# K tile 1 of the first projection is issued from ACT's queue instead of SP's

## The chip, the cores and the metric

One Trainium2 chip, one core of it. The metric is the device time of one execution in microseconds (us), the median of several runs. The kernel before takes 143.43 us (three runs, 143.29 to 143.65).

PE is the matrix engine (TensorE; PEld its weight loads), DVE the vector engine, ACT the scalar engine, POOL GpSimd, SP the engine that issues most DMAs. The small q behind an engine's name (SPq, ACTq, POOLq) marks its sequencer, which issues DMAs, waits for semaphores and hands instructions to the engine.

## The reference

One layer of a hybrid decoder with 256 tokens of width 1024, in float32:

```
h = rms_norm(x, norm_g)
mq, mk, mv, mg, dq, dk, dv, dg = split(h @ w_in)          # eight chunks of 512 columns
m_out = block_attention(norm(mq), norm(mk), mv) * silu(mg) # 8 heads of 64, ALiBi, causal
d_out = rms_norm(diff_attention(norm(dq), norm(dk), dv)) * 0.8 * silu(dg)
x + concat(m_out, d_out) @ w_out
```

## The kernel before

The input is used transposed: eight k tiles of 128 rows, each 256 columns wide (the tokens). Every float32 operand is split into a high and a low part (`whi`, `wlo` for weights, `xhi`, `xlo` for the input), and each product is three matmuls: high by high, high by low, low by high (`PASSES`). The order of all work is written out by hand in the table `ORDER`: steps `x.0` to `x.7` split the first eight k tiles, `u.0` to `u.7` are the matmuls of the first chunk (dq), one k tile each, `h.`, `l.` and `L.` split and load the later weights, the rest is attention and the output projection.

The first chunk comes in with the input. Array `xw` holds for each k tile 128 rows with 256 columns of x and 512 columns of dq's weights. The x part of tile 0 lies in the array `small_x` beside the norm gains, and is the first DMA of all (L103). Tile 0's weights come in two halves of 256 columns (L110), tiles 1 to 7 whole, 768 columns, 384 KB each (L112). All DMAs are issued by SP, in the order of the code. Of the DMAs that the names DMAHW0 to DMAHW7 stand for, in rotation, a later one that takes the same name waits for the earlier one to land.

For every tile kt, `split_first` does this: DVE (for tiles 3, 5, 7 ACT) makes `xhi` (L156 or L154), DVE makes `xlo` (L157), ACT makes `whi` (L265), DVE makes `wlo` (L266); tile 0's weights go in two halves. Then `unit_nat` issues the matmuls (L293): tile 0 twelve of 256 columns, the other tiles six of 512.

Ahead of them stand a memset on DVE (L124) and one exponential on ACT (L125), which brings in ACT's table, and seven warm-up matmuls on zeros (L131; each is two instructions). Two more of these, the fillers, stand behind the matmuls of tile 0. POOL meanwhile makes eight bias tiles (L144).

Behind dq come the chunks dk, dv and so on, whose weights are loaded by `load_w` (L250) into three buffers and split at L273 and L277.

Of the kernel before, what the change touches and what calls it, by code (L numbers as in the profile page):

```python
# [55 lines left out]
def kernel(  # L56
# [9 lines left out]
    nc = tc.nc  # L66
# [12 lines left out]
    def bank(name):  # L79
        tag = free_banks.pop(0)  # L80
        t = psum.tile([P, 512], F32, tag=tag, name=name)
        bank_of[id(t)] = (tag, t)
        return t
# [7 lines left out]
    def tile768(name):  # L91
        tag = free_tiles.pop(0)
        t = work.tile([P, 768], F32, tag=tag, bufs=1, name=name)
        tile_of[id(t)] = (tag, t)
        return t
# [9 lines left out]
    first = []  # L105
    for kt in range(KT):
        t = tile768("first")
        if kt == 0:
            for c in (slice(S, 512), slice(512, 768)):
                nc.sync.dma_start(out=t[:, c], in_=xw[kt][:, c])  # L110
        else:
            nc.sync.dma_start(out=t, in_=xw[kt][:, 0:768])  # L112
        first.append(t)
    xn = const.tile([P, 2, D], F32, name="xn")
# [8 lines left out]
    warm = const.tile([P, 1], F32, name="warm")  # L123
    nc.vector.memset(warm, 0.0)  # L124
    nc.scalar.activation(out=warm, in_=warm, func=AF.Exp)  # L125
    zero = nc.const_aps.tensor(0.0, [P, 512], F32)
    wps = bank("warm_ps")

# [566 lines left out]
```

## Time and profile before

| what | us |
|---|---|
| median of three runs | 143.43 |
| the profiled execution, its own time | 142.81 |
| its span, first to last instruction | 141.0 |
| PE busy | 137.1 (97%) |
| DVE busy | 105.8 (75%) |
| ACT busy | 84.2 (60%) |
| POOL busy | 23.3 (17%) |
| DMA, mean over the span | 173 GB/s |

The profiled execution's own time holds its span and 1.8 us around it. The profile page gives for each engine the union of its instructions' times; the chain of waits is followed back from the last instruction; the timeline lists an engine's instructions in order, merged where they stand on one line, and in brackets the idle time before each and what ended it. Times are us from the start of the span. A merged row's time reaches from the first start to the last end; matmuls overlap, so their pitch is read from one start to the next.

### The profile page before, as it was taken

How to read it: one execution, taken by the hardware profiler on the slowest of the kernel's cores; microseconds unless marked ns; L12 is line 12 of the kernel's file. 1: busy time of each engine (PE TensorE's matmuls, PEld its weight loads, DVE VectorE, ACT ScalarE, POOL GpSimd, SP SyncE). 2: the span in 40 equal slices, each digit the busy share in tenths (PEclk: the TensorE clock that was granted, in tenths of full speed). 3: DMA queues.
4: the chain of work that ended last, by engine and by line, in shares of the span. 5: the costliest groups of instructions: out<-in, count | busy, mean ns of one | idle time of the engine just before them, and what ended most of it. 6: DMA issues, size and time to landing. Idle time of an engine off the chain costs nothing.

```text
span 141.0 us, 2227 instructions
## 1 busy us (share of the span) xinstructions
PE 137.1 (97%) x806; PEld 116.5 (83%) x806; DVE 105.8 (75%) x249; ACT 84.2 (60%) x167; POOL 23.3 (17%) x28
## 2 busy tenths in 40 slices
PE   7999999999999999999999999999999999999991
PEld 7978888887888888888877888888999888898890
DVE  1799985989995998997999999994529435692331
ACT  4378893694292998945640599799768504670000
POOL 7970000000000000000000000279760007000000
PEclk9999999999999999999999999999999999999999
DMA  5999999571809600268960004916144800000232
GB/s 117 303 410 413 409 426 407 237 246 56 297 0 316 281 2 0 30 272 293 328 274 0 0 0 121 414 65 225 72 112 191 297 0 0 7 0 0 81 142 74
DMA packets 5482, 24.39 MB, mean 173 GB/s; under 512 B 608, under 2 KB 1376, under 8 KB 3424
## 3 DMA queue, kind: packets, MB, share of 16 engines
q1 hardware_dynamic: 5472, 24.26, 47.3%
q8 instruction: 6, 0.10, 0.3%
q14 instruction: 4, 0.03, 0.1%
HBM read 23.21 MB, written 1.05 MB: 172 GB/s over the span
## 4 chain that ended last, share of the span: by engine, by line
PE 97%; DVE 0%; issue 0%
PE oacc L602 16%; PE acc_dq L293 9%; PE acc_mg L308 8%; PE acc_mq L293 8%; PE acc_dg L293 8%; PE acc_mk L293 8%; PE acc_dv L293 8%; PE acc_mv L293 8%; PE acc_dk L293 8%; PE s_ps L413 4%; PE T_ps L318 3%; PE warm_ps L131 3%; PE mo_ps L495 2%; PE do_ps L501 1%; PE aT_ps L473 1%; PE aT_ps L471 1%
## 5 line engine op out<-in xcount | busy, mean ns | idle before, releaser
L277 DVE TENSOR_TENSOR wlo<-w,whi 128x1024 fp32r<-128x1024 f32 x36 | 43.5, 1232 | 6.0 <-ACT whi L273 5.7
L273 ACT ACTIVATE whi<-w 128x1024 fp32r<-128x1024 f32 x36 | 36.4, 1057 | 4.4 <-DMA w<-w 4.1
L443 POOL TENSOR_TENSOR p<-p,rs 128x512 f32<-128x512 f32 (+1 forms) x8 | 8.3, 1064 | 82.0 <-DVE rs L439 81.7
L433 ACT ACTIVATE p<-p,nmax 128x256 f32<-128x256 f32 (+1 forms) x32 | 14.1, 443 | 3.9 <-DVE nmax L423 3.9
L423 DVE CUSTOM_DVE_ANT_0 p<-s_ps,bias 128x256 f32<-128x256 f32 (+1 forms) x32 | 9.1, 351 | 1.8 <-PE s_ps L413 1.8
L602 PE MATMUL oacc<-whi,mixm 128*128 128x512 f32 (+1 forms) x40 | 10.4, 347 | 0.0
L602 PE MATMUL oacc<-whi,mixd 128*128 128x512 f32 (+1 forms) x40 | 10.4, 346 | 0.0
L308 PE MATMUL acc_mg<-xhi,whi 128*128 128x256 f32 x32 | 9.2, 289 | 0.0
L308 PE MATMUL acc_mg<-xlo,whi 128*128 128x256 f32 x32 | 9.0, 281 | 0.0
L308 PE MATMUL acc_mg<-xhi,wlo 128*128 128x256 f32 x32 | 9.0, 281 | 0.0
L609 DVE TENSOR_TENSOR o<-oacc,xn 128x512 f32<-128x512 f32 (+1 forms) x5 | 2.9, 585 | 7.7 <-PE oacc L602 7.7
L602 PEld LDWEIGHTS oacc<-whi,mixm 128*128 128x128 f32 x40 | 7.1, 189 | 1.0
L602 PEld LDWEIGHTS oacc<-whi,mixd 128*128 128x128 f32 x40 | 7.0, 188 | 1.0
L144 POOL TENSOR_SCALAR bias<-dist 128x256 f32<-128x256 f32 x8 | 7.3, 922 | 0.4
L265 ACT ACTIVATE whi<-first 128x512 fp32r<-128x512 f32 (+1 forms) x9 | 5.0, 577 | 3.7 <-DMA first<-xw 3.7
L602 PE MATMUL oacc<-wlo,mixd 128*128 128x512 f32 (+1 forms) x20 | 6.9, 347 | 0.0
L602 PE MATMUL oacc<-wlo,mixm 128*128 128x512 f32 (+1 forms) x20 | 6.9, 347 | 0.0
L479 ACT ACTIVATE pT<-aT_ps 128x512 f32<-128x512 f32 x6 | 3.6, 594 | 5.4 <-PE aT_ps L472 5.4
L293 PE MATMUL acc_mk<-whi,xhi 128*128 128x512 f32 x16 | 6.7, 418 | 0.0
L293 PE MATMUL acc_mv<-whi,xhi 128*128 128x512 f32 x16 | 6.5, 405 | 0.0
L293 PE MATMUL acc_dv<-whi,xhi 128*128 128x512 f32 x16 | 6.5, 405 | 0.0
L293 PE MATMUL acc_dg<-whi,xhi 128*128 128x512 f32 x16 | 6.5, 404 | 0.0
(167 smaller groups left out, 352.8 us busy)
## 6 DMA issues: line engine op xcount, KB each, us to landing
w<-w SPq DMA_DIRECT2D x16, 1024.0 KB, 4.9
first<-xw SPq DMA_DIRECT2D x7, 384.0 KB, 5.7
w<-w SPq DMA_DIRECT2D x4, 512.0 KB, 8.5
xn<-x SPq DMA_DIRECT2D x2, 512.0 KB, 9.5
out<-o SPq DMA_DIRECT2D x3, 256.0 KB, 2.1
first<-xw SPq DMA_DIRECT2D x2, 128.0 KB, 2.6
out<-o SPq DMA_DIRECT2D x2, 128.0 KB, 1.7
small<-small_x SPq DMA_DIRECT2D x1, 136.0 KB, 2.3
```

The source lines that it names most:

```text
L131: nc.tensor.matmul(wps[:, 0:P], lhsT=zero[:, 0:P], rhs=zero[:, 0:P], start=True, stop=True)
L144: nc.gpsimd.tensor_scalar(out=b, in0=dist, scalar1=2.0 ** -(h + 1), scalar2=None, op0=ALU.mult)
L265: nc.scalar.activation(out=hi[:, c], in_=src, func=AF.Copy)
L273: nc.scalar.activation(out=piece(i)[0], in_=raw_half(i), func=AF.Copy)
L277: nc.vector.tensor_tensor(out=lo, in0=raw_half(i), in1=hi.bitcast(F32), op=ALU.subtract)
L293: nc.tensor.matmul(acc[name][t][:, o:o + n], lhsT=(xhi, xlo)[a][:, kt, t * P:(t + 1) * P], rhs=wp[b][:, c:c + n], start=kt == 0 and i == 0 ...
L308: nc.tensor.matmul(acc[name][j // 2][:, (j % 2) * S:(j % 2 + 1) * S], lhsT=wp[b][:, c:c + P], rhs=(xhi, xlo)[a][:, kt], start=kt == 0 and ...
L413: nc.tensor.matmul(ps[c][k][:, o:o + n], lhsT=qk[g + "q"][a][rows, pr, q0:q0 + P], rhs=qk[g + "k"][b][rows, pr, 0:n], start=i == 0, stop=i ...
L423: nc.vector.tensor_tensor_reduce(out=p[:, o:o + n], in0=s_ps[g][c][k][:, b:b + n], in1=biases[c][:, S - n:], scale=-1.0, scalar=3.0e38, op ...
L433: nc.scalar.activation(out=p[:, o:o + n], in_=p[:, o:o + n], func=AF.Exp, scale=-1.0, bias=mx[:, i:i + 1], accum_out=sums[g, pr][:, i:i + 1])
L443: nc.gpsimd.tensor_tensor(out=p3, in0=p3, in1=q.unsqueeze(2).to_broadcast([P, 2, n]), op=ALU.mult)
L602: nc.tensor.matmul(acc["o", c][j][:, 0:n], lhsT=qk[g][a][:, kt, t * P:(t + 1) * P], rhs=pieces[piece][b][:, o:o + n], start=first and i == ...
```

## The change

SP no longer issues tile 1; ACT does, on its own queue. In the code the issue stands behind the exponential of L125. SP issues tile 2 where it issued tile 1 before, and each later tile one place earlier.

```diff
         if kt == 0:
             for c in (slice(S, 512), slice(512, 768)):
                 nc.sync.dma_start(out=t[:, c], in_=xw[kt][:, c])
-        else:
+        elif kt > 1:
             nc.sync.dma_start(out=t, in_=xw[kt][:, 0:768])
         first.append(t)
...
     nc.vector.memset(warm, 0.0)
     nc.scalar.activation(out=warm, in_=warm, func=AF.Exp)
+    nc.scalar.dma_start(out=first[1], in_=xw[1][:, 0:768])
     zero = nc.const_aps.tensor(0.0, [P, 512], F32)
```

Lines from 126 on stand one further down in the changed kernel.

ACT's instructions from the start of the program, before; `warm` is the scratch value of the exponential, `first` a k tile, and in brackets stands what an instruction waits for (DVE_49 is a count of DVE's work, DMAHW1_49 the landing of the DMA with that name):

```order
L125 ACT_TABLE_LOAD
L125 ACTIVATE warm<-warm 128x1 [waits DVE_49]
L265 ACTIVATE whi<-first 128x256 [waits DMAHW1_49]
L265 ACTIVATE whi<-first 128x256 [waits DMAHW2_49]
L265 ACTIVATE whi<-first 128x512 [waits DMAHW3_49]
L265 ACTIVATE whi<-first 128x512 [waits DMAHW4_49]
```

The same place in the changed kernel:

```order
L125 ACT_TABLE_LOAD
L125 ACTIVATE warm<-warm 128x1 [waits DVE_49]
L126 DMA first<-xw 128x768
L266 ACTIVATE whi<-first 128x256 [waits DMAHW1_49]
L266 ACTIVATE whi<-first 128x256 [waits DMAHW2_49]
L266 ACTIVATE whi<-first 128x512 [waits DMAHW4_49]
L266 ACTIVATE whi<-first 128x512 [waits DMAHW3_49]
```

The DMA is the third instruction and waits for nothing of its own. Tile 1 now has the name DMAHW4, tile 2 DMAHW3.

SP's DMAs from the start of the program, before:

```order
L103 DMA small<-small_x 128x272
L110 DMA first<-xw 128x256 x2
L112 DMA first<-xw 128x768 x5
L112 DMA first<-xw 128x768 [waits DMAHW0_49]
L112 DMA first<-xw 128x768 [waits DMAHW1_49]
L250 DMA w_172<-w 128x1024 [waits DMAHW2_49]
L250 DMA w_172<-w 128x1024 [waits DMAHW3_49]
L250 DMA w_175<-w 128x1024 [waits DMAHW4_49]
```

And in the changed kernel:

```order
L103 DMA small<-small_x 128x272
L110 DMA first<-xw 128x256 x2
L112 DMA first<-xw 128x768 x4
L112 DMA first<-xw 128x768 [waits DMAHW0_49]
L112 DMA first<-xw 128x768 [waits DMAHW1_49]
L251 DMA w_172<-w 128x1024 [waits DMAHW2_49]
L251 DMA w_172<-w 128x1024 [waits DMAHW3_49]
L251 DMA w_175<-w 128x1024 [waits DMAHW4_49]
```

SP issues one tile less. The second half of the first w load waits for DMAHW3, which was tile 1 and is tile 2 now; the next one waits for DMAHW4, which was tile 2 and is tile 1 now.

## Rows read from the trace of the kernel before

**Rows 1.** Stretches: length, busy PE, PEld, DVE, ACT, POOL, granted clock, DMA share, GB/s.
```profile
16.78:137.89 121.11, 121.07 (x734) 102.93 (x733) 92.64 (x225) 73.63 (x151) 14.66 (x12) 1.00 0.42 154
```

**Rows 2.** The chain of waits, first 18 us: start, length, what.
```profile
0.75 3.32 PE warm_ps L131 x14
...
6.58 10.20 PE acc_dq L293 x42
```

**Rows 3.** PE's timeline: start, length, engine, line, operation, count.
```profile
4.39 0.63 PE L293 MATMUL acc_dq<-whi,xlo 128*128 128x256 f32 x2
4.82 0.56 PE L293 MATMUL acc_dq<-wlo,xhi 128*128 128x256 f32 x2
...
5.72 0.40 PE L293 MATMUL acc_dq<-wlo,xhi 128*128 128x256 f32 x2
5.96 0.61 PE L131 MATMUL warm_ps<-const-float32-0.0 128*128 128x128 f32 x4
...
6.29 0.27 PE L131 MATMUL warm_ps<-const-float32-0.0 128*128 128x128 f32 x1
6.58 0.73 PE L293 MATMUL acc_dq<-whi,xhi 128*128 128x512 f32 x2
...
9.62 0.62 PE L293 MATMUL acc_dq<-whi,xhi 128*128 128x512 f32 x2
...
12.42 0.39 PE L293 MATMUL acc_dq<-whi,xhi 128*128 128x512 f32 x1
```

**Rows 4.** Waits of PE's weight loads, first 18 us: total, times, longest.
```profile
PEld acc_dq L293 <- DVE wlo L266: 0.5, 2, 0.3
PEld acc_dq L293 <- ACT whi L265: 0.2, 1, 0.2
```

**Rows 5.** DVE's timeline, first 8 us.
```profile
0.79 0.06 DVE L124 MEMSET warm<- 128x1 f32 x1 [0.79 <-PEq L687]
...
5.91 0.37 DVE L156 TENSOR_SCALAR xhi<-first,small 128x256 fp32r<-128x256 f32 x1 [0.35 <-DMA first<-xw]
...
6.71 0.88 DVE L266 TENSOR_TENSOR wlo<-first,whi 128x512 fp32r<-128x512 f32 x1
```

**Rows 6.** ACT's timeline, first 8 us.
```profile
0.71 1.28 ACT L125 ACT_TABLE_LOAD   x1 [0.71 <-PEq L687]
2.00 0.20 ACT L125 ACTIVATE warm<-warm 128x1 f32<-128x1 f32 x1
...
5.90 0.63 ACT L265 ACTIVATE whi<-first 128x512 fp32r<-128x512 f32 x1 [0.81 <-DMA first<-xw]
7.37 0.63 ACT L265 ACTIVATE whi<-first 128x512 fp32r<-128x512 f32 x1 [0.84 <-DMA first<-xw]
```

**Rows 7.** L691's sequencer step (ns; first and last start, us) and ACT's timeline, late.
```profile
L691 ACTq DRAIN  x2: 14/1900/3787, 122.2 to 140.6; - x2
122.04 3.89 ACT L273 ACTIVATE whi<-w 128x1024 fp32r<-128x1024 f32 x4
98.01 1.28 ACT L582 ACT_TABLE_LOAD   x1
99.31 1.27 ACT L582 ACTIVATE sg<-acc_dg,r 128x512 f32<-128x512 f32 x2
```

**Rows 8.** SP's issues of tiles 1 to 7, and tile 1's us from issue to landing.
```profile
2.08 3.60 SPq L112 DMA_DIRECT2D first<-xw  x7
first<-xw SPq DMA_DIRECT2D x1, 384.0 KB, 3.8
```

**Rows 9.** Busy time by stretches, columns as in rows 1.
```profile
1.50:4.50 3.00, 3.00 (x16) 2.99 (x15) 1.47 (x3) 1.11 (x3) 2.84 (x5) 1.00 0.89 203
6.58:16.78 10.20, 10.20 (x43) 7.96 (x44) 10.10 (x19) 7.58 (x12) 2.99 (x4) 1.00 1.03 411
```

**Rows 10.** Timelines of DVE and PE at the first w load.
```profile
14.82 3.64 DVE L277 TENSOR_TENSOR wlo<-w,whi 128x1024 fp32r<-128x1024 f32 x3
16.85 0.39 PE L293 MATMUL acc_dk<-wlo,xhi 128*128 128x512 f32 x1
```

## The prediction, made before the change was run

> **What bounds the kernel now.** TensorE (PE) is busy 97% of the span; the table by stretches says where the rest is: from 16.78 to 137.89 us PE works 121.07 of 121.11 us [rows 1], so no later wait can take up a shift. What the first 16.78 us gain or lose, the end gains or loses. The chain of waits there is PE alone: the warm-up matmuls to 4.07 us, tile 0 of dq, two fillers, and then 10.20 us for tiles 1 to 7 [rows 2]. In PE's timeline a pair of 512-wide matmuls takes 0.467 us once things run (six pairs from 9.62 to 12.42 us), while tiles 1 and 2, six pairs too, take from 6.58 to 9.62 us, 3.04 us instead of 2.80 [rows 3]. The waits of PE's weight loads name the holes: 0.2 us for tile 1's high half (ACT, L265), 0.5 us for two low halves (DVE, L266) [rows 4].
>
> Behind both stands one transfer. DVE ends tile 0 at 5.56 us and then sits 0.35 us until tile 1 has landed, which it starts at 5.91 us [rows 5]; ACT starts tile 1's high half at 5.90 us after 0.81 us idle for a DMA [rows 6]. DVE's three steps for tile 1 follow each other to 7.59 us and those of tile 2 come straight behind, so the delay is handed on.
>
> **The prize.** PE's fillers start 0.11 us apart (three steps from 5.96 to 6.29 us), so PE could go on at 6.40 us instead of 6.58: 0.18 us. The holes in tiles 1 and 2 are 3.04 - 2.80 = 0.24 us. Together 0.42 us, all that an early tile 1 can give as long as tile 0 comes when it does now. An early tile 1 does close them: with DVE on tile 1 straight from 5.56 us, its steps (5.91 to 7.59 us now, 1.68 us [rows 5]) end at 7.24 us, and PE, from 6.40 us, wants the low half two pairs later, at 7.33 us.
>
> **When ACT issues it.** The new instruction stands third in ACT's stream, behind the table load (0.71 to 1.99 us) and the exponential (2.00 to 2.20 us) [rows 6]. What counts is whether ACT's sequencer waits for these two to end. The trace says no. At the end of the program ACT's sequencer starts its closing DRAIN at 122.2 us, and it lasts 3787 ns, while four activations of L273 run from 122.04 to 125.93 us [rows 7]: the sequencer had passed three that had not begun. And the activation behind the second table load starts at 99.31 us, 0.02 us after the load's end: it had been handed over before. The exponential waits only for DVE's memset, done at 0.85 us [rows 5]. So the issue falls near 0.9 us, beside SP's issues of small and tile 0, which end before 2.08 us [rows 8], and not at 2.20 us. An issue took SP 0.51 us (seven in 3.60); ACT's next work waits for tile 0 to land, so the issue costs ACT nothing.
>
> **When tile 1 lands then.** From SP's queue it took 3.8 us from issue to landing, behind small and tile 0 [rows 8]. If it takes as long, it lands at 4.7 us; with a queue of its own it can only be earlier than that by the part that it spent behind them. DVE wants it at 5.56 us: hidden, with 0.86 us of cover. Tile 2 takes tile 1's place in SP's issue, one issue earlier than now, and should land before the 7.37 us at which ACT starts it now; DVE then waits neither in tile 1 nor in tile 2.
>
> **What it takes from tile 0.** Tile 1's 384 KB now move beside small and tile 0, 392 KB. From both sides: if they fit into idle capacity, tile 0 is not late at all: from 1.50 to 4.50 us the engines moved 203 GB/s against 411 later [rows 9], so 3.0 us x 208 = 624 KB were free, more than the 393 KB (thousand bytes) wanted; against that, the engines counted as busy for 0.89 of it, with packets that waited. If all of tile 1 goes ahead, tile 0 is late by 393 KB / 411 GB/s = 0.96 us. The first half of tile 0 will feel it more: I take 0.6 us there, PE's first real matmul at about 4.4 us instead of 3.8. PE then has two pairs at the early pitch of 0.43 us (4.39 to 4.82) and four at the later one of 0.24 (5.72 to 5.96) [rows 3], done at 4.4 + 0.86 + 0.96 = 6.2 us where now the fillers begin at 5.96. So 0.2 us, nearer the lower end because the bytes leave room. DVE's low half of tile 0's second half may come as much late, beside it and not on top.
>
> [...] No row here shows two loading queues at once. [...]
>
> Of the rest: the bytes and the computing instructions stay the same. SP's later issues wait for other landings: the second half of the first w load for tile 2 instead of tile 1, the next one for tile 1 instead of tile 2. They are not near: the low half of the very first w tile starts on DVE at 14.82 us and takes 1.2 us (three in 3.64), and PE asks for it at 16.85 us [rows 10], 0.8 us of cover, more than the 0.42 us that PE can come earlier. With that cover gone PE would wait for DVE at the first dk tile.
>
> **The sum.** -0.18 - 0.24 + 0.2 = -0.22 us: 142.81 becomes 142.6 us for a profiled execution like this one. That execution lies 0.62 us under the median of the runs (143.43), so the median becomes 143.2 us. With tile 0 late by 0 to 0.96 us it is 143.0 to 144.0 us. What a measurement of this kernel can tell from no change is about 0.3%, 0.43 us: the whole prize has that size, and my forecast is a difference that can't be told.
>
> **Rival 1, slower: the issue does wait for the table load and the exponential.** Then it starts at 2.20 us, 0.12 us later than now (2.08 us [rows 8]), while tile 2 is issued at 2.08 us on the other queue and moves beside it. PE reaches tile 1 between 0.12 us later than now and the time at which both have come, where now tile 2's high half starts: 7.37 - 5.90 = 1.47 us [rows 6]. I take 1.2, nearer the upper end: two tiles asked for at the same time share the engines, and these counted as busy for 0.89 of the time even with one [rows 9]. DVE's chain moves along whole, so nothing is won back: 144.0 us, 144.6 on the median's scale. It decides from an issue at about 1.76 us on: 3.8 us later, at 5.56 us, DVE wants the tile. For it: the order in the code. Against it: rows 7. Chance 0.17.
>
> **Rival 2, slower: the clock.** [...] Chance 0.08.
>
> **Rival 3, faster: tile 0 is not late at all**, or even earlier, as its last packets no longer have tile 1 behind them in SP's queue. Then 0.42 us or a little more: 142.4 us, or 143.0 and less on the median's scale. For it: the free bytes [rows 9]. Chance 0.10.
>
> **How the numbers follow.** The forecast has 0.65, its own range 143.0 to 144.0 us. Faster by over 0.3%: most of rival 3 and the lowest part of the forecast, 0.19. Slower: rivals 1 and 2 nearly whole and the uppermost part of the forecast, 0.27. Within: 0.54. The range reaches down to 142.8 (rival 3 with 0.2 us more) and up to 144.7, which holds rivals 1 and 2 at the values taken; outside are their worse ends.
>
> **What would show it.** ACT's DMA issue near 0.9 us (2.2: rival 1); ACT's high half of tile 1 right behind that of tile 0; no wait of DVE before tile 1 and none of PE's weight loads on L266 in tiles 1 and 2; tiles 1 to 7 in about 9.9 us instead of 10.20; the first real matmul 0.3 to 1.0 us later than now; the dk matmul of 16.85 us at about 16.6. I am wrong if tile 1 lands after 5.6 us, if tile 0's second half comes more than 0.5 us late, or if tile 1's pairs run at 0.9 us.

## The result and the profile after

The changed kernel takes 144.83 us (median of 12 runs, 143.17 to 145.31), the kernel before, run beside it on the same chip, 143.17 us (12 runs, 142.67 to 143.65). The ratio is 1.0102, 95% interval 1.008 to 1.0123: 1% slower, 1.5 us, above the predicted range. Medians here are of all runs, ratios go by the means of the runs in the chip's fast state, so the two can differ by a few tenths of a percent. The loss is not in every run: three of the twelve lie at 143.17 to 143.43 us, beside the kernel before, the other nine at 144.00 to 145.31. The profiled execution of the changed kernel took 144.45 us, with a span of 142.7 us, against 142.81 and 141.0.

First the stretch that must not have changed, busy time by engine of the changed kernel (columns as in rows 1; its first dk matmul comes 1.65 us later than before: 18.27 instead of 16.62):

```profile
18.43:139.50 121.07, 121.06 (x735) 102.93 (x733) 91.68 (x223) 72.86 (x150) 14.65 (x12) 1.00 0.41 146
```

PE is as dense there as in [rows 1]. All that was lost was lost before 18.43 us. The chain of waits of the first 20 us (start, length, what) says with whom:

```profile
1.15 3.39 DMA first<-xw
...
4.56 0.42 ACT whi L266
...
5.03 2.93 PE acc_dq L294 x12
7.96 0.67 PE warm_ps L132 x4
8.63 9.80 PE acc_dq L294 x42
```

In [rows 2] the chain was PE from 0.75 us on. Now it runs through a transfer: the first half of tile 0's weights, issued by SP at 1.15 us, landed at 4.54 us. ACT's timeline shows the rest of that story (ACTq is its DMA issue):

```profile
0.71 1.28 ACT L125 ACT_TABLE_LOAD   x1 [0.71 <-PEq L688]
0.89 0.38 ACTq L126 DMA_DIRECT2D first<-xw  x1
...
4.56 0.42 ACT L266 ACTIVATE whi<-first 128x256 fp32r<-128x256 f32 x1 [2.35 <-DMA first<-xw]
5.50 0.94 ACT L266 ACTIVATE whi<-first 128x256 fp32r<-128x256 f32 x2 [0.52 <-DMA first<-xw]
```

The issue of tile 1 ran at 0.89 us, in the middle of the table load that stands ahead of it. The merged row at 5.50 us holds tile 0's second half and tile 1's high half, one behind the other. The issues and their us to landing, changed kernel (of the two L110 issues at 1.15 and 1.62 us the first row is the first half):

```profile
first<-xw ACTq DMA_DIRECT2D x1, 384.0 KB, 3.3
small<-small_x SPq DMA_DIRECT2D x1, 136.0 KB, 2.5
first<-xw SPq DMA_DIRECT2D x1, 128.0 KB, 3.4
first<-xw SPq DMA_DIRECT2D x1, 128.0 KB, 3.9
```

Tile 1 landed at 0.89 + 3.3 = 4.2 us. The first half of tile 0 took 2.2 us before and 3.4 now, the second 3.0 and 3.9. What the two queues moved (packets, MB, share of the 16 engines; q10 is ACT's, q1 SP's), from 2.4 to 3.4 us, then from 2.87 to 3.50 us, where SP's queue moved nothing, and from 3.4 to 4.4 us:

```profile
q10 hardware_dynamic: 102, 0.31, 81.9%
q1 hardware_dynamic: 79, 0.07, 20.5%
...
q10 hardware_dynamic: 80, 0.25, 97.8%
...
q1 hardware_dynamic: 273, 0.27, 84.6%
q10 hardware_dynamic: 42, 0.08, 20.6%
```

From 2.4 to 3.4 us the engines moved 0.31 of tile 1's 0.39 MB; what SP's queue moved beside it, 0.07 MB, was the rest of `small`. Tile 0's first half moved only behind that, from 3.50 us on. Tile 1 was issued 0.26 us ahead of tile 0's first half, and its bytes went ahead of it. What held the first half back, the engines or the way from the issue to them, no view here separates. The engines did use idle capacity: 278 GB/s from 1.50 to 4.50 us, where they moved 203 [rows 9]. It just was not tile 0 that got it. And PE's timeline, changed kernel:

```profile
5.03 0.80 PE L294 MATMUL acc_dq<-whi,xhi 128*128 128x256 f32 x2 [0.95 <-ACT whi L266]
5.62 0.63 PE L294 MATMUL acc_dq<-whi,xlo 128*128 128x256 f32 x2
6.05 0.63 PE L294 MATMUL acc_dq<-wlo,xhi 128*128 128x256 f32 x2
6.48 0.63 PE L294 MATMUL acc_dq<-whi,xhi 128*128 128x256 f32 x2
6.91 0.63 PE L294 MATMUL acc_dq<-whi,xlo 128*128 128x256 f32 x2
7.33 0.63 PE L294 MATMUL acc_dq<-wlo,xhi 128*128 128x256 f32 x2
7.76 0.87 PE L132 MATMUL warm_ps<-const-float32-0.0 128*128 128x128 f32 x4
8.38 0.71 PE L294 MATMUL acc_dq<-whi,xhi 128*128 128x512 f32 x2
8.94 0.63 PE L294 MATMUL acc_dq<-whi,xlo 128*128 128x512 f32 x2
```

PE stood idle for 0.95 us behind the warm-ups. The pairs of tile 0 then start 0.43 us apart (the first 0.59, as it takes 0.60 in the kernel before), the lower level of the clock, and only the pairs of tile 1 run at the higher one (8.94 to 9.41 us, 0.47 us for 512 columns). In [rows 3] the change of level fell between 4.82 and 5.72 us, 3 us earlier. The packed traces also keep the moment from which the clock is granted at 1.00, which no view prints: 5.16 us before, 8.31 us in the changed kernel. From start to start the loss adds up: the first real matmul 1.24 us later (3.79 to 5.03), tile 0 up to the fillers 0.56 us longer (2.73 instead of 2.17), the fillers the same, and tiles 1 to 7, up to the first dk matmul, 0.15 us shorter (9.89 instead of 10.04): 1.65 us.

### The profile page after: what moved, and what is told of

It is laid out like the page before. It is cut to its first block, busy times and chain, and to the rows that moved or that the text cites. A ratio compares the mean times of both kernels' runs of the same rounds, so it can differ in the third digit from the quotient of the medians.

```text
span 142.7 us, 2227 instructions
## 1 busy us (share of the span) xinstructions
PE 137.8 (97%) x806; PEld 117.5 (82%) x806; DVE 105.9 (74%) x249; ACT 83.9 (59%) x167; POOL 23.2 (16%) x28
## 4 chain that ended last, share of the span: by engine, by line
PE 94%; DMA 2%; DVE 0%; ACT 0%; SPq 0%; issue 0%
PE oacc L603 16%; PE acc_dq L294 9%; PE acc_mg L309 8%; PE acc_mq L294 8%; PE acc_dg L294 8%; PE acc_mk L294 8%; PE acc_dv L294 8%; PE acc_mv L294 8%; PE acc_dk L294 8%; PE s_ps L414 4%; PE T_ps L319 3%; DMA first<-xw 2%; PE mo_ps L496 2%; PE do_ps L502 1%; PE aT_ps L474 1%; PE aT_ps L472 1%
## 5 line engine op out<-in xcount | busy, mean ns | idle before, releaser
L267 DVE TENSOR_TENSOR wlo<-first,whi 128x512 fp32r<-128x512 f32 (+1 forms) x9 | 6.0, 671 | 1.3 <-ACT whi L266 1.3
L294 PE MATMUL acc_dq<-whi,xhi 128*128 128x512 f32 (+1 forms) x18 | 5.9, 414 | 0.9 <-ACT whi L266 0.9
```

What stands on the lines that cost most here:

```text
L267: nc.vector.tensor_tensor(out=lo[:, c], in0=src, in1=hi[:, c].bitcast(F32), op=ALU.subtract)
L294: nc.tensor.matmul(acc[name][t][:, o:o + n], lhsT=(xhi, xlo)[a][:, kt, t * P:(t + 1) * P], rhs=wp[b][:, c:c + n], start=kt == 0 and i == 0 ...
```

## The experiments

My theory (A) after the result: tile 0 comes late because tile 1's bytes go ahead of it; this costs some tenths by itself, and most of the loss is that PE's gap in front of tile 0 delays the rise of the clock. The rival (B): the late landing costs 1.6 us by itself, and the late rise of the clock has another cause than the gap. Each run is compared with runs of the kernel before on the same chip; different runs can be on different chips, so two of them are compared by their ratios. The edits are of the line `N_WARM, N_FILL, N_TILES = 7, 2, 9` where nothing else is shown.

**Close the gap in the changed kernel.**

```diff
-N_WARM, N_FILL, N_TILES = 7, 2, 9
+N_WARM, N_FILL, N_TILES = 9, 2, 9
```

> The change, with 9 warm-up matmuls instead of 7, so that PE is busy until about 5.0 us, when tile 0 lands. Theory A (the changed kernel loses mostly because PE's gap between warm-ups and tile 0 delays the rise of the clock): the rise comes back to about 5.2 us, matmuls of tile 0 run at 0.23 us a pair soon after, and the time falls to 143.5 to 143.8 us, ratio 1.002 to 1.005 to the kernel before. Theory B (tile 0's late landing costs 1.6 us by itself): the time stays at 144.8 us, ratio 1.01.

Measured: 143.64 us, ratio 1.0034 (1.002 to 1.0048). The loads are as late as in the changed kernel, but in PE's timeline the pace is back:

```profile
5.16 0.51 PE L294 MATMUL acc_dq<-whi,xhi 128*128 128x256 f32 x2 [0.23 <-ACT whi L266]
5.50 0.40 PE L294 MATMUL acc_dq<-whi,xlo 128*128 128x256 f32 x2
5.74 0.40 PE L294 MATMUL acc_dq<-wlo,xhi 128*128 128x256 f32 x2
```

Two more matmuls on zeros took 1.2 us off by the medians, 0.7% or 1.0 us by the ratios. In the traces the first real matmul comes 0.13 us later than in the changed kernel (5.16 us), the first dk matmul 1.0 us earlier (17.27 us). As A expected; B falls.

**The same late start without the change's DMAs:** the kernel before with 9 warm-ups, the same edit.

> The kernel before, with 9 warm-up matmuls, which push PE's first real matmul from 3.8 to about 5.0 us, as late as in the changed kernel, with all DMAs as before and no gap. Theory A: the clock rises as before, PE catches up at the higher level, and the time is within 0.2% of before. Theory B (a first matmul at 5.0 us costs by itself): 1 us or more slower.

Measured: 142.98 us, ratio 0.9992 (0.9978 to 1.0005). A first real matmul 0.8 us late (4.59 us in its timeline, behind the warm-ups) cost nothing here, where PE did not stand still in front of it and the loads were on time: PE's weight loads had been waiting 0.7 us in tiles 1 and 2 anyway [rows 4].

**The gap without the change's DMAs:** the kernel before with 4 warm-ups.

```diff
-N_WARM, N_FILL, N_TILES = 7, 2, 9
+N_WARM, N_FILL, N_TILES = 4, 2, 9
```

> The kernel before, with 4 warm-up matmuls, which end at about 2.65 us and leave PE idle for 1.1 us ahead of the first real matmul at 3.8 us; DMAs as before. Theory A (a gap of this size delays the rise): slower by 0.5 to 1.7 us, matmuls of tiles 0 and 1 at the lower level. Theory B (only the landing counts): no change, within 0.2%.

Measured: 144.16 us, ratio 1.0061 (1.0034 to 1.0088). The first real matmul comes at 3.77 us, as before; PE's timeline:

```profile
3.77 0.80 PE L293 MATMUL acc_dq<-whi,xhi 128*128 128x256 f32 x2 [0.97 <-DVE xlo L157]
4.37 0.63 PE L293 MATMUL acc_dq<-whi,xlo 128*128 128x256 f32 x2
...
7.21 1.20 PE L293 MATMUL acc_dq<-whi,xhi 128*128 128x512 f32 x2
8.21 0.90 PE L293 MATMUL acc_dq<-whi,xlo 128*128 128x512 f32 x2
8.95 0.62 PE L293 MATMUL acc_dq<-wlo,xhi 128*128 128x512 f32 x2
```

A gap of 0.97 us, as long as the one of the changed kernel, and the lower level lasts to about 8.8 us, into tile 1. So late loads are not needed for it. Four warm-ups are also less work ahead of tile 0 than seven; against that as the cause speaks the changed kernel, which has the same seven as the kernel before, and the late rise with its gap. Here too the loss is not in every run: four of the twelve lie at 143.18 to 143.55 us.

**What is left of the loss:** the change with 9 warm-ups and without fillers (`9, 0, 9`).

> The change with 9 warm-up matmuls and without the two fillers behind tile 0. Tile 1 now lies ready when tile 0's matmuls end, so the fillers, 0.44 us of PE, bridge nothing. Theory A: the time falls by 0.4 us against the same kernel with fillers (143.64), to about 143.2 us, the time of before. If the fillers still hide a wait for tile 1's parts: no gain, 143.6 us.

Measured: 142.99 us, ratio 1.0004 (0.9989 to 1.002). With the gap closed and the fillers gone, the change costs nothing, and gains nothing. The fillers cost because tile 1 was already there: 0.3% by the ratios, 0.43 us, as expected (the medians, from two chips, lie 0.65 us apart).

**The fillers alone:** the change with 7 warm-ups and none of them (`7, 0, 9`).

> The change with its 7 warm-ups, without the two fillers. The gap ahead of tile 0 stays, so the late rise of the clock stays (1.2 us by the runs with 9 warm-ups); the fillers' 0.87 us (at the lower level) fall away. Theory A: 144.83 - 0.65 to 0.87, about 144.0 to 144.2 us, still about 1 us slower than before. If the fillers were the loss, and not the gap: 143.0 to 143.3 us.

Measured: 144.52 us, ratio 1.0077 (1.0045 to 1.011): 0.3 us less than with them, which the two intervals do not separate from nothing, and not 0.65 to 0.87. The timeline, of an execution of 144.92 us, shows why:

```profile
7.89 1.06 PE L294 MATMUL acc_dq<-whi,xhi 128*128 128x512 f32 x2
8.75 1.05 PE L294 MATMUL acc_dq<-whi,xlo 128*128 128x512 f32 x2
9.60 0.86 PE L294 MATMUL acc_dq<-wlo,xhi 128*128 128x512 f32 x2
```

Here tile 1 itself ran at the lower level, a pair in 0.86 us. What the fillers did not spend there, real work spent.

**The kernel before, 9 warm-ups, no fillers** (`9, 0, 9`).

> The kernel before (all loads on SP) with 9 warm-up matmuls and no fillers. With 9 warm-ups PE reaches the end of tile 0 at 6.75 us, after tile 1's high half is there (about 6.55 us), so the fillers only cost. Theory A: 142.6 to 142.8 us, 0.2 to 0.4 us faster than before, and faster than the change in any form. If PE then runs into DVE's low half of tile 1 instead: 143.0 us, no difference.

Measured: 142.95 us, ratio 0.9992 (0.9978 to 1.0006). No difference: in the profiled execution the clock rose early (the pairs of tile 0 start 0.23 us apart from 4.76 us on), PE was through tile 0 at about 6.1 us, and its weight loads waited 0.5 us for tile 1's high half, which is what fillers are for, and later 0.4 us for tile 2's low one.

**The issue behind the exponential, my rival 1 as a kernel** (the edit is against the changed kernel).

```diff
+    nc.scalar.activation(out=first[1][:, 0:1], in_=warm, func=AF.Exp)
     nc.scalar.dma_start(out=first[1], in_=xw[1][:, 0:768])
```

> The change with a second exponential that writes one column of tile 1, so that ACT's issue has to wait for it and comes at about 2.3 us. Queue theory (a DMA's data are served in about the order of issue, over both queues): small and tile 0 land as in the kernel before (2.98, 3.30, 4.66 us), tile 2 goes first and tile 1 lands at about 7 us; PE waits for it, 1.0 to 1.4 us slower than before, 144.1 to 144.6 us. If the lateness of tile 0 came from the mere use of two queues, tile 0 is late here too.

Measured: 146.65 us (four runs, 144.93 to 147.48), ratio 1.0211 (1.016 to 1.0262), well beyond the expectation. ACT issued at 2.47 us; small and tile 0's second half were as early as before (4.5 us for the half), the first half came 0.3 us later than before (3.6 us) though nothing of ACT's queue had yet moved. So using two queues did not by itself make tile 0 as late as it is in the changed kernel, and 0.3 us is what the landing varied by here. Tile 2, issued at 2.09 us, landed 4.9 us later, at 7.0 us, and tile 1 at 2.47 + 6.0 = 8.5 us: the earlier issue was done first. Stretches of this run, columns as in rows 1:

```profile
6.60:9.20 2.60, 0.00 (x1) 0.01 (x1) 0.65 (x2) 0.69 (x2) 2.48 (x3) 1.00 1.02 396
9.20:10.60 1.40, 1.40 (x6) 1.13 (x7) 1.36 (x4) 1.40 (x4) 0.02 (x1) 1.00 1.04 417
10.60:14.00 3.40, 3.40 (x10) 2.62 (x9) 3.36 (x8) 3.18 (x7) 0.00 (x0) 0.50 1.03 414
```

PE stood still for 2.6 us, went on at the higher level for 1.4 us, and then got half the clock (0.50) for 3.4 us while it was busy, its pairs 0.85 us apart (10.77 to 11.62 us) instead of 0.46: in this trace the half clock came behind the wait, not in it.

**A third of the bytes:** ACT loads only the x columns of tile 1, SP its weights (against the changed kernel).

```diff
-        elif kt > 1:
-            nc.sync.dma_start(out=t, in_=xw[kt][:, 0:768])
+        else:
+            c = slice(S if kt == 1 else 0, 768)
+            nc.sync.dma_start(out=t[:, c], in_=xw[kt][:, c])
...
-    nc.scalar.dma_start(out=first[1], in_=xw[1][:, 0:768])
+    nc.scalar.dma_start(out=first[1][:, 0:S], in_=xw[1][:, 0:S])
```

> Only the 256 x columns of tile 1 (128 KB) go to ACT's queue at 0.9 us; its weights (256 KB) stay on SP. Queue theory: tile 0 is late by a third of what it was late in the changed kernel (first half 1.24 us there, here about 0.4, landing at about 3.7 us), the gap ahead of PE's first real matmul is about 0.1 us, and the time is 143.0 to 143.4 us, as before. If the lateness does not go by the bytes put ahead: the first half lands after 4.2 us and the time is 144 us or more.

Measured: 143.41 us, ratio 1.0027 (1.0011 to 1.0042). The landings (ACT's issue at 0.89, SP's at 1.15, 1.63 and 2.09 us):

```profile
first<-xw ACTq DMA_DIRECT2D x1, 128.0 KB, 2.5
first<-xw SPq DMA_DIRECT2D x1, 128.0 KB, 2.6
first<-xw SPq DMA_DIRECT2D x1, 128.0 KB, 3.8
first<-xw SPq DMA_DIRECT2D x1, 256.0 KB, 4.9
```

The first half took 2.6 us instead of 2.2 before and 3.4 in the change: a lateness that goes by the bytes put ahead would look like this (0.4 and 1.2 us for 128 and 384 KB), but 0.4 us is little more than the 0.3 us of the run above, so the proportion is not shown. The second half, at 3.8 us, is nearly as late as in the change, which this does not explain. PE stood still for 0.72 us within tile 0, at 5.2 to 6.0 us, when the clock had risen already, and the pairs behind that gap kept the pitch of the higher level (0.24 us).

**Tile 0's first half on ACT instead of tile 1** (against the kernel before).

```diff
-            for c in (slice(S, 512), slice(512, 768)):
-                nc.sync.dma_start(out=t[:, c], in_=xw[kt][:, c])
+            nc.sync.dma_start(out=t[:, 512:768], in_=xw[kt][:, 512:768])
...
+    nc.scalar.dma_start(out=first[0][:, S:512], in_=xw[0][:, S:512])
```

> Instead of tile 1, the first half of tile 0's weights (128 KB) goes to ACT's queue at about 0.9 us; SP issues small, the second half, then tiles 1 to 7. If what lands first is what was issued first, over both queues, the first half lands at about 3.1 us instead of 3.3, the second about 4.2, tile 1 about 5.4, PE's first matmul comes 0.2 us earlier, and the time is 0.3 to 0.5 us less than before. If a second queue is only a nuisance (its transfer and SP's get in each other's way): no gain, 143.2 us or more.

Measured: 143.06 us, ratio 1.0 (0.9984 to 1.0015). No gain: issued 0.26 us earlier, the half took 2.7 us beside small, which was on its way, and landed at 3.6 us, 0.3 us later than before. There was no gap behind the warm-ups, and yet the clock rose only at 6.47 us by the packed trace, behind nearly all of tile 0 (its pairs start 0.43 us apart up to 6.40 us). With 8 warm-ups and no fillers on top (`8, 0, 9`):

> The first half of tile 0's weights on ACT's queue (as in the run before with that), 8 warm-ups so that no gap is left ahead of PE's first real matmul at about 4.5 us, and no fillers, since tile 1 lands at 5.5 us. The clock rises in unbroken work and nothing is filled: 142.5 to 142.8 us, 0.2 to 0.4 us faster than before. If what bounds the start is how much of PE's work falls at the lower level, which none of this changes: 143.0 us, no difference.

Measured: 143.48 us, ratio 1.0013 (0.9988 to 1.0037). A miss: in its profiled execution tiles 1 and 2 were late (6.2 and 8.3 us), and PE's weight loads waited 1.8 us for ACT's high halves; without fillers the wait lay bare.

**Both queues, each for what is wanted first:** ACT issues tile 0's first half and then tile 1 ahead of its table load, SP small, the second half, and tile 2 on; `8, 0, 9` (against the kernel before).

```diff
-            for c in (slice(S, 512), slice(512, 768)):
-                nc.sync.dma_start(out=t[:, c], in_=xw[kt][:, c])
+            for c, e in ((slice(S, 512), nc.scalar), (slice(512, 768), nc.sync)):
+                e.dma_start(out=t[:, c], in_=xw[kt][:, c])
         else:
-            nc.sync.dma_start(out=t, in_=xw[kt][:, 0:768])
+            e = nc.scalar if kt == 1 else nc.sync
+            e.dma_start(out=t, in_=xw[kt][:, 0:768])
```

> Both queues share the first loads in the order in which they are wanted: ACT issues the first half of tile 0 and then tile 1, ahead of its table load (0.7 and 1.2 us); SP issues small, the second half of tile 0 and tile 2 on. 8 warm-ups, no fillers. Queue theory (served in about the order of issue): tile 0's halves land at about 3.6 and 4.0 us, tile 1 at about 5.2, tile 2 at 6.3; nothing is late for PE and the time is 142.4 to 142.8 us. If tile 1 goes ahead of tile 0's second half again: that half lands after 4.7 us, and the time is 143.2 us or more.

Measured: 142.61 us, ratio 0.9961 (0.9941 to 0.998): faster than the kernel before, and within the expectation, though the halves landed later than it said (4.0 and 4.7 us). And with the kernel's own 7 warm-ups and 2 fillers:

> The loads shared by both queues as in the run before, with the kernel's own 7 warm-ups and 2 fillers, so that only the DMAs differ from the kernel before. PE's first real matmul comes at about 4.5 us, after a gap of 0.4 us behind the warm-ups, and the fillers cost 0.4 us although tile 1 has landed. Theory A: 143.0 to 143.5 us, no gain or a little slower; the gain of the run before needs the warm-ups and fillers to fit. If the gain is the DMAs' alone: 142.6 us.

Measured: 142.59 us, ratio 0.9957 (0.9936 to 0.9977). My expectation missed: the gain is the DMAs' alone. PE's timeline of this run:

```profile
0.76 3.33 PE L132 MATMUL warm_ps<-const-float32-0.0 128*128 128x128 f32 x14 [0.76 <-PEq L688]
3.99 0.76 PE L294 MATMUL acc_dq<-whi,xhi 128*128 128x256 f32 x2
```

and its issues of tile 0's first half (ACT, 0.71 us), second half (SP, 1.15 us) and tile 1 (ACT, 1.14 us):

```profile
first<-xw ACTq DMA_DIRECT2D x1, 128.0 KB, 2.8
first<-xw SPq DMA_DIRECT2D x1, 128.0 KB, 3.5
...
first<-xw ACTq DMA_DIRECT2D x1, 384.0 KB, 3.8
```

No gap was left, since the first half landed at 3.5 us. Tile 1 lands at 4.9 us instead of 5.88, and tile 0's second half, issued at the same moment, still comes at 4.7 us as it did before. The profiled executions lie only 0.1 us apart (142.70 and 142.81), while the medians differ by 0.5 us in one comparison and 0.8 us in the other; where the executions of the kernel before lose the rest, one trace each cannot show, and it stays open. The runs do show that the times lie closer together: 142.45 to 143.00 us here, 142.66 to 144.04 for the kernel before beside it.

## Why the prediction was wrong

Right: PE alone bounds the stretch behind the first 17 us, and a shift there goes to the end unchanged. ACT's issue runs ahead of the engine: 0.89 us, predicted 0.9, though the table load ends at 1.99. Tile 1 landed at 4.2 us, before the 4.7 given as the latest. The holes in tiles 1 and 2 closed for the most part: the two tiles took 2.89 us (8.38 to 11.27), where they had taken 3.04 and 2.80 was hoped for. DVE started tile 1 straight behind tile 0, and there is no wait of PE's weight loads on L267; DVE's timeline of the changed kernel shows it, against the 0.35 us of [rows 5]:

```profile
5.95 0.52 DVE L267 TENSOR_TENSOR wlo<-first,whi 128x256 fp32r<-128x256 f32 x1 [0.41 <-ACT whi L266]
6.39 0.40 DVE L157 TENSOR_SCALAR xhi<-first,small 128x256 fp32r<-128x256 f32 x1
```

Tiles 1 to 7 take 9.80 us in the chain, against 10.20 [rows 2] and a predicted "about 9.9", but the chain's row begins 0.25 us behind their first matmul; from start to start 0.15 us was won. One of the signs named for being wrong came: tile 0's second half was 0.8 us late (5.5 us), more than 0.5.

The step that failed is "What it takes from tile 0". Two terms of it were wrong:

- The lateness. I took 0.6 us for the first half, between 0 and 0.96 us, and chose low "because the bytes leave room". It was 1.2 us, above the upper bound: that took 411 GB/s, while tile 1 moved at 0.31 MB a microsecond, and at that pace its 393 KB take 1.27 us. The capacity was free, but it was tile 1 that filled it. I priced it as if tile 0 and tile 1 shared the engines, which no row showed; the queue counts show tile 1 served nearly whole before tile 0: from 2.87 to 3.50 us 80 of its packets moved, and nothing of SP's queue. By what rule the engines took them in this order, no run shows.
- The clock. I let PE do two pairs at 0.43 us and four at 0.24; all six ran at 0.43. So rival 2, the clock, came true, to which I gave 0.08. The 1.4 us with which it entered the range is shown by no run; what closing the gap gave back was 1.0 to 1.2 us. The sign I named for it, pairs of 0.9 us in tile 1, did not come (0.47 us): the slow pairs were those of tile 0 and the fillers. With the first matmul at 4.4 us and the warm-ups done at 4.07 us the gap was short, 0.3 us, where it was 0.95. The two errors are one: here the lateness made the gap, and behind the gap the higher clock came at 8.31 us instead of 5.16. I gave them separate chances and never worked out rival 2 for the upper bound of the lateness.

Split by the runs, the loss of 1.0% is 0.7% for the gap (ratio 1.0102 with 7 warm-ups, 1.0034 with 9) and 0.3% for fillers that no longer bridge anything (1.0034 with them, 1.0004 without). The late start costs nothing beyond that: with 9 warm-ups and no fillers the first real matmul comes at 4.97 us, nearly as late as in the changed kernel, and the time is that of before. So what the gap costs is the slow matmuls behind it. The gap alone, made in the kernel before with 4 warm-ups, costs 0.6%, by the same slow pairs. Of the prize of 0.42 us the trace shows 0.15 us, in tiles 1 and 2; the 0.18 us at the fillers, which took 0.62 us as before, was not collected in the changed kernel.

Rival 1 was priced at 1.2 us slower; made as a kernel it is 2.1% slower, some 3 us: tile 1 landed behind tile 2, PE idled 2.6 us for it and then ran at half the clock for 3.4 us.

## What to carry to other kernels

A load put on a second queue did not run beside the first queue for free here: 0.31 MB of tile 1, issued 0.26 us ahead, moved before tile 0's first half did. So ask which smaller, earlier-wanted transfer is issued just behind it, and put the early-wanted one first on each queue. At the start of a kernel price the gap that a late load leaves in PE together with the clock: here a gap of 0.95 us cost mostly by the slow matmuls behind it, and two more matmuls on zeros bought 0.7 of the 1.0% back. When a wait moves, the fillers set for the old wait have to move with it.

## What the runs showed of the hardware that was not expected

A DMA in ACT's stream was issued at 0.89 us, while ACT's table load ran from 0.71 to 1.99 us. A 384 KB transfer issued 0.26 us ahead of a 128 KB one on the other queue had 0.31 of its 0.39 MB moved before the other began to, from 3.50 us on, while two of the same sizes issued at the same moment (1.14 and 1.15 us, the run with both queues and 7 warm-ups) landed at 4.9 and 4.7 us. In the three kernels with a gap of about 1 us in PE behind the warm-ups, between 2.7 and 5.2 us, the higher clock came at 8.31 us (the changed kernel), 8.80 us (4 warm-ups before) and 10.11 us (the changed kernel without fillers), by the moments kept in the packed traces. In the eleven with a gap of at most 0.26 us there it came at 6.47 us at the latest, in the kernel before at 5.16 us. That is one execution each, and the moment varies even without a gap; in the kernels with the gap, a quarter to a third of the runs took no longer than the slowest of the kernel before, and when their clock rose is not recorded. A gap of the same size behind the rise did not cost the clock: with tile 0's first half on ACT, 8 warm-ups and no fillers, PE idled for 0.92 us up to 6.96 us, and tile 1 ran at the higher level (a pair in 0.48 us). After 2.6 us of standing still PE was granted 0.50 not during the wait but from 10.60 us on, 1.4 us into its work. The views print the granted clock of the first microseconds as 1.00 throughout, so that in them the level there can be read from the pitch of the matmuls only.
